# Pinning the order of three engines in the input norm, and splitting the load of the constants

## Chip, cores and metric

The kernel runs on one core of a Trainium2 chip. The metric is the device time of one execution in microseconds (us), the median of several runs. The engines are named as in the profile: PE is TensorE, PEld its weight loads, DVE is VectorE, ACT is ScalarE, POOL is GpSimd, SP is SyncE (here it only issues DMAs).

## What is computed

One layer of a bidirectional encoder on 512 tokens of width 1024, in float32. Cut to its frame, the reference is:

```python
x = x + token_mixer(rmsnorm(x, norm_mix), w_in, ...)
x = x + cross_attention(rmsnorm(x, norm_xattn), rmsnorm(mem, norm_mem), ...)
x = x + squared_relu_mlp(rmsnorm(x, norm_mlp), w_up, w_down)
return rmsnorm(x, norm_final)

def rmsnorm(x, g):
    y = x * lax.rsqrt(jnp.mean(x * x, axis=-1, keepdims=True) + 1e-6)
    return y * g
```

The change touches only the first line: the RMS norm of the input ahead of the token mixer, and the loads that go with it. The mixer begins with one large input projection, `proj = rmsnorm(x) @ w_in + b_in`; its columns are the values, queries, forget gates and so on of two groups of recurrent heads.

## The kernel before

**Number format.** Every large product is made of three products. Each operand is split into a high part (a copy rounded to the fast matmul format, made by ScalarE) and a low part (the rest, made by VectorE: source minus high part). `split_out` (L222) writes both; `mm3` (L226) multiplies high by high (L227), high by low (L228) and low by high (L229) into one PSUM bank. So every operand costs one pass of ScalarE and one of VectorE before TensorE can use it.

**Weights.** All weight matrices lie in DRAM as blocks of 128 x 1024 in the order of use (`SEQ`). `load` (L198) fetches a block through SyncE's queue into one of three buffers `st`; `split` (L205) makes its high and low parts (`wh`, `wl`, three buffers each). `weights` (L214) hands out a block and asks for the splits of the next two and the load of a third.

**The input norm (L288 to L304).** The tokens come in four tiles of 128 x 1024 (`xtile`, in the trace `as`), loaded by SyncE with the first two weight blocks between them (L134, L202). For each tile ScalarE squares it and sums the rows (L292, with a short instruction that reads the accumulator), VectorE turns the sum into a mean (L167), and GpSimd raises it to the power -0.5 (L169; `rstd_of`). VectorE then scales each half of the tile by that and by the gain row (L297). The gain row stands in two PSUM banks, `gmix`, into which TensorE multiplied it at the start (L143). TensorE transposes each half in four blocks of 128 x 128 into PSUM (L300), using the identity `ident`, and `split_out` makes the high and low halves of the transposed tile `xT` (L302). The first weight blocks are split after tiles 0 and 1 (L304).

**The first projection (L317, `proj_t`, L253).** It takes four weight blocks, each covering two of the eight 128-row blocks of the width, and all four token tiles: 4 x 4 x 2 x 3 = 96 products of 128 x 128 by 128 x 512. The first three weight blocks go through all tiles one after the other; the last goes tile by tile. The gate projection follows (L462, with the operands the other way round in the trace: `mm<-xT,wh` instead of `mm<-wh,xT`).

**Small constants.** `cs` (128 x 392) holds the identity (columns 0 to 127), two masks and a selector; it is loaded in one DMA from ScalarE's queue (L138). `vc` (128 x 117) holds biases, gains and convolution weights, and `lm` is a mask kept as bytes, which is loaded as floats and converted. Both are handled in `small_setup` (L145), after the four tiles, by DMAs from SyncE's queue (L147, L148), a VectorE copy for the mask (L149), and some instructions on 8 columns (L152 to L159). The mask is used by the masked copy at L383, the biases after the gate projection (L468 onwards).

**What sets the order.** Except in the last part of the kernel (the MLP, where TensorE's order is the program's), the order of the instructions on each engine is chosen by a planner: it plays the program through with estimated times and takes what it believes to be ready first, earlier lines and lines under `tc.high_priority()` before others. On the chip each engine then keeps to its list, and waits at the head of it. Only L294 to L302 and the later weight splits have high priority in this stage.

Of the kernel before, what the change touches and what calls it, by code (L numbers as in the profile page):

```python
# [13 lines left out]
AF = mybir.ActivationFunctionType  # L14
ALU = mybir.AluOpType
# [3 lines left out]
P = 128  # L19
S = 512  # L20
D = 1024
# [18 lines left out]
C_ID, C_MF, C_MB, C_SEL, NC1 = 0, 128, 256, 384, 392  # L40
C_INC, C_SUF, C_ISUF, C_PRE, C_ONE = 0, 128, 256, 384, 512
NC_ = NC1 + 640
LEVELS = (1, 2, 4, 8, 16, 32, 64)
# [36 lines left out]
def trunk(ctx: ExitStack, tc: tile.TileContext, x, mem, wpk, vec, cst, lmask, rmask, rows, out):  # L80
    nc = tc.nc
# [4 lines left out]
    v, sc, gp, pe = nc.vector, nc.scalar, nc.gpsimd, nc.tensor  # L86
    cnt = [0]

    def nm(s):
        cnt[0] += 1  # L90
        return f"{s}_{cnt[0]}"

    def T(tag, w, bufs, dt=F32):
        return (sb if w == 516 else big).tile([P, w], dt, tag=tag, name=nm(tag), bufs=bufs)

    def mmb():
        return psm.tile([P, 512], F32, tag="mm", name=nm("mm"))

    def smb():
        return pss.tile([P, 512], F32, tag="sm", name=nm("sm"))  # L100

    def tiny(w):
        return sb.tile([P, w], F32, tag=f"tiny{w}", name=nm("tiny"), bufs=2 if w == 8 else 6)

    def ap(t, off, *dims):
        a = t[:, :]
        return bass.AP(a.tensor, a.offset + off, [list(a.ap[0])] + [list(d) for d in dims])
# [12 lines left out]
    cs = sb.tile([P, NC1], F32, name="cs")  # L120
    vc = sb.tile([P, NV], F32, name="vc")
    lm = sb.tile([P, len(LEVELS) * P], U8, name="lm")
    ident = cs[:, C_ID:C_ID + P]
    grow1 = RG()
    xin = [A16(), A16()]
    xtile = [xin[t // 2][:, (t % 2) * 1024:(t % 2) * 1024 + 1024] for t in range(4)]
# [8 lines left out]

    load_x(0)
    nc.scalar.dma_start(out=grow1[0:1, :], in_=rows[0:1, :])
    nc.scalar.dma_start(out=cs, in_=cst[:, 0:NC1])  # L138
    one1 = misc[0:1, 63:64]
    gp.memset(one1, 1.0)  # L140
    gmix = [mmb(), mmb()]
# [2 lines left out]

    def small_setup():  # L145
        lmf = A4()
        nc.sync.dma_start(out=vc, in_=vec)  # L147
        nc.sync.dma_start(out=lmf[:, 0:len(LEVELS) * P], in_=lmask)  # L148
        v.tensor_copy(lm, lmf[:, 0:len(LEVELS) * P])  # L149
        le, lr = tiny(8), tiny(8)  # L150
        lg = vc[:, V_LB:V_LB + 8]
        v.tensor_tensor(out=le, in0=lg, in1=lg, op=ALU.subtract)  # L152
        sc.activation(le, le, AF.Exp)
        v.reciprocal(lr, le)
        v.tensor_tensor(out=le, in0=le, in1=lr, op=ALU.mult)
        v.tensor_tensor(out=lb[:, 0:8], in0=le, in1=le, op=ALU.subtract)
        v.tensor_scalar(out=lb[:, 8:16], in0=lb[:, 0:8], scalar1=-1.0, scalar2=1.0, op0=ALU.mult, op1=ALU.add)
        v.tensor_copy(selr, cs[:, C_SEL:C_SEL + 8])
        v.tensor_scalar(out=negb, in0=vc[:, V_FF:V_FF + 8], scalar1=-1.0, scalar2=None, op0=ALU.mult)  # L159
# [5 lines left out]
    def rstd_of(ss, w, n):  # L165
        ms = tiny(w)
        v.tensor_scalar(out=ms, in0=ss, scalar1=1.0 / n, scalar2=EPS, op0=ALU.mult, op1=ALU.add)  # L167
        r = tiny(w)
        gp.tensor_tensor(out=r, in0=ms, in1=nh.to_broadcast([P, w]), op=ALU.pow)  # L169
        return r, ms  # L170
# [27 lines left out]
    def load(i):  # L198
        if i >= NSTREAM or i in st_tiles:
            return  # L200
        t = T("st", 1024, 3)
        nc.sync.dma_start(out=t, in_=wpk[i])  # L202
        st_tiles[i] = t

    def split(i):  # L205
        if i >= NSTREAM or i in hl_tiles:
            return
        load(i)
        s = st_tiles[i]
        hi, lo = T("wh", 1024, 3, F32R), T("wl", 1024, 3, F32R)  # L210
        split_out(hi, lo, s)
        hl_tiles[i] = (hi, lo)
# [9 lines left out]
    def split_out(dst_hi, dst_lo, src):  # L222
        sc.activation(dst_hi, src, AF.Copy)  # L223
        v.tensor_tensor(out=dst_lo, in0=src, in1=dst_hi.bitcast(F32), op=ALU.subtract)  # L224
# [7 lines left out]
    def xk(tiles, n=512):  # L232
        o = []
        for k in range(8):
            t = tiles[k // 4]
            b = (k % 4) * 2 * n
            o.append((t[:, b:b + n], t[:, b + n:b + 2 * n]))
        return o

    def proj_d(mat, c0, xs, n=512, count=2):  # L240

        for j in range(count):
            wh, wl = weights(("d", mat, 0, c0 + P * j))
            ps = mmb()
            for k in range(8):
                z = slice(k * P, k * P + P)
                mm3(ps[:, :n], wh[:, z], wl[:, z], xs[k][0], xs[k][1], k == 0, k == 7)
                if k == 3:
                    tick()
            yield ps  # L250
            tick()
# [29 lines left out]
    xT = XT()  # L281
# [4 lines left out]
    load_x(3)  # L286

    junk = G4()  # L288
    for t in range(4):
        xt = xtile[t]  # L290
        ss = tiny(1)
        sc.activation(junk, xt, AF.Square, accum_out=ss)  # L292
        r, _ = rstd_of(ss, 1, D)
        with tc.high_priority():  # L294
            for g in range(2):
                xg = xt[:, g * 512:g * 512 + 512]
                v.scalar_tensor_tensor(out=xg, in0=xg, scalar=r, in1=gmix[g], op0=ALU.mult, op1=ALU.mult)  # L297
                ps = smb()
                for k in range(4):
                    pe.transpose(ps[:, k * P:k * P + P], xg[:, k * P:k * P + P], ident)  # L300
                p3 = ps[:, :].rearrange("p (k t) -> p k t", t=P)
                split_out(ap(xT[g], t * P, [1024, 4], [1, P]), ap(xT[g], 512 + t * P, [1024, 4], [1, P]), p3)  # L302
        if t < 2:
            split(t)  # L304
    small_setup()
    xs = xk(xT)


# [397 lines left out]
    for t in range(2):  # L706
# [6 lines left out]
        ss = tiny(1)  # L713
        v.tensor_tensor(out=ss, in0=s2_[:, 0:1], in1=s2_[:, 1:2], op=ALU.add)
        r, _ = rstd_of(ss, 1, D)
# [6 lines left out]
    for k in range(8):  # L722
        ps = smb()
        for t in range(2):
            pe.transpose(ps[:, t * P:t * P + P], mt[t][:, k * P:k * P + P], ident)
        g = vc[:, V_MEM + k:V_MEM + k + 1]
# [217 lines left out]
    for f in range(4):  # L944
# [3 lines left out]
        for p in range(4):  # L948
            a = []
            for j in range(2):  # L950
                ps, = proj_d("up", 1024 * f + P * (p + 4 * j), x3, count=1)
# [65 lines left out]
        while n < len(JOBS):  # L1017
            p, g = JOBS[n]
# [104 lines left out]
```

## Time and profile before

| | |
|---|---|
| median of 3 runs | 877.57 us (877.56 to 878.74) |
| the profiled execution | 877.47 us |
| its span, first to last instruction | 875.7 us |
| TensorE busy | 853.6 us (97%) |
| VectorE busy | 576.2 us (66%) |
| ScalarE busy | 415.5 us (47%) |
| GpSimd busy | 67.4 us (8%) |

Busy time of TensorE counts pipelined products whose ends are modelled, so the pace of the products (start to start) tells more than their length: 0.39 us each in the rows, but one starts every 0.227 us. Times in the timeline are counted from the start of the span. In a row of the timeline the first number is the start, the second the length of the group that the row merges; `x2` is the number of instructions; what stands in brackets is the idle time of the engine before it and what ended that. `out<-in` names the tiles by the program's names.

### The profile page before, as it was taken

How to read it: one execution, taken by the hardware profiler on the slowest of the kernel's cores; microseconds unless marked ns; L12 is line 12 of the kernel's file. 1: busy time of each engine (PE TensorE's matmuls, PEld its weight loads, DVE VectorE, ACT ScalarE, POOL GpSimd, SP SyncE). 2: the span in 40 equal slices, each digit the busy share in tenths (PEclk: the TensorE clock that was granted, in tenths of full speed). 3: DMA queues.
4: the chain of work that ended last, by engine and by line, in shares of the span. 5: the costliest groups of instructions: out<-in, count | busy, mean ns of one | idle time of the engine just before them, and what ended most of it. 6: DMA issues, size and time to landing. Idle time of an engine off the chain costs nothing.

```text
span 875.7 us, 11191 instructions
## 1 busy us (share of the span) xinstructions
PE 853.6 (97%) x4198; PEld 709.3 (81%) x4198; DVE 576.2 (66%) x1006; ACT 415.5 (47%) x758; POOL 67.4 (8%) x114
## 2 busy tenths in 40 slices
PE   7999999999999999999999999999999999999995
PEld 5887888888887886888888887888888888888884
DVE  5557688779536987654655445776667656766675
ACT  5235343353358658534544355553355345435544
POOL 2000000010001000000000200002200310121001
PEclk9999999999999999999999999999999999999998
DMA  7322222311234223352212772238945993598322
GB/s 261 135 98 79 73 73 73 117 63 50 73 99 117 97 98 120 121 169 84 85 51 71 194 190 82 92 116 212 284 143 127 238 279 109 150 284 217 115 55 96
DMA packets 32680, 113.58 MB, mean 130 GB/s; under 512 B 3761, under 2 KB 3889, under 8 KB 32626
## 3 DMA queue, kind: packets, MB, share of 16 engines
q1 hardware_dynamic: 23120, 78.84, 26.1%
q0 software_dynamic: 9216, 33.56, 17.2%
q8 instruction: 33, 0.54, 0.2%
q10 hardware_dynamic: 290, 0.47, 0.1%
q14 instruction: 21, 0.17, 0.1%
HBM read 110.76 MB, written 2.10 MB: 129 GB/s over the span
## 4 chain that ended last, share of the span: by engine, by line
PE 49%; DVE 1%; ACT 0%; POOL 0%; issue 0%; POOLq 0%; ACTq 0%
PE mm L228 10%; PE mm L229 10%; PE mm L227 10%; PE sm L997 5%; PE sm L999 5%; PE sm L998 5%; PE mm L999 1%; PE mm L998 1%; PE mm L997 1%; PE sm L229 1%; PE sm L228 1%; PE sm L227 1%; PE sm L770 0%; PE sm L827 0%; DVE vv L922 0%; ACT t L756 0%
## 5 line engine op out<-in xcount | busy, mean ns | idle before, releaser
L223 ACT ACTIVATE wh<-st 128x1024 fp32r<-128x1024 f32 x133 | 140.9, 1059 | 233.1 <-PE mm L228 115.4
L224 DVE TENSOR_TENSOR wl<-st,wh 128x1024 fp32r<-128x1024 f32 x133 | 162.7, 1223 | 124.3 <-ACT wh L223 120.6
L227 PE MATMUL mm<-xT,wh 128*128 128x512 f32 x552 | 219.7, 399 | 0.0
L228 PE MATMUL mm<-xT,wh 128*128 128x512 f32 x552 | 216.4, 392 | 0.2 <-DVE xT L776 0.2
L229 PE MATMUL mm<-xT,wl 128*128 128x512 f32 x552 | 215.8, 391 | 0.0
L228 PEld LDWEIGHTS mm<-xT,wh 128*128 128x128 f32 x552 | 103.8, 188 | 22.7 <-DVE xT L776 2.0
L229 PEld LDWEIGHTS mm<-xT,wl 128*128 128x128 f32 x552 | 103.6, 188 | 21.7 <-issue 0.2
L227 PEld LDWEIGHTS mm<-xT,wh 128*128 128x128 f32 x552 | 103.8, 188 | 21.4 <-issue 1.2
L891 POOL DMA_DIRECT2D as<-in_wpk x48 | 36.6, 772 | 312.1 <-DVE wl L224 188.1
L955 DVE SCALAR_TENSOR_TENSOR t<-mm,rg 128x512 f32<-128x512 f32 x32 | 22.1, 691 | 55.2 <-PE mm L229 55.0
L229 PE MATMUL mm<-wh,yT 128*128 128x512 f32 x128 | 50.6, 395 | 0.0
L227 PE MATMUL mm<-wh,yT 128*128 128x512 f32 x128 | 50.5, 394 | 0.0
L228 PE MATMUL mm<-wl,yT 128*128 128x512 f32 x128 | 50.0, 391 | 0.0
L999 PE MATMUL sm<-wh,yT 128*128 128x512 f32 x128 | 49.8, 389 | 0.0
L998 PE MATMUL sm<-wl,yT 128*128 128x512 f32 x128 | 49.8, 389 | 0.0
L997 PE MATMUL sm<-wh,yT 128*128 128x512 f32 x128 | 49.8, 389 | 0.0
L223 ACT ACTIVATE wh<-as 128x1024 fp32r<-128x1024 f32 x24 | 25.5, 1062 | 33.3 <-PE sm L999 23.7
L224 DVE TENSOR_TENSOR wl<-as,wh 128x1024 fp32r<-128x1024 f32 x24 | 29.4, 1225 | 13.9 <-ACT wh L223 13.9
L378 PEld LDWEIGHTS sm<-a,t 128*128 128x128 f32 x224 | 30.1, 191 | 2.2 <-ACT t L368 0.4
L930 DVE TENSOR_TENSOR vv<-vv,sm 128x512 f32<-128x512 f32 x48 | 31.0, 680 | 1.2 <-PE sm L999 1.2
L368 ACT ACTIVATE t<-a 128x512 f32<-128x512 f32 x28 | 18.4, 674 | 26.3 <-DVE a L431 23.8
L378 PE MATMUL sm<-a,t 128*128 128x128 f32 x224 | 30.9, 285 | 0.0
(258 smaller groups left out, 1513.5 us busy)
## 6 DMA issues: line engine op xcount, KB each, us to landing
st<-in_wpk SPq DMA_DIRECT2D x133, 512.0 KB, 3.3
as<-in_wpk POOLq DMA_DIRECT2D x48, 512.0 KB, 6.7
gate<-in_wpk POOLq DMA_DIRECT2D x16, 512.0 KB, 7.2
as<-in_x SPq DMA_DIRECT2D x4, 512.0 KB, 6.5
vv<-in_x SPq DMA_DIRECT2D x8, 256.0 KB, 4.3
out<-vv SPq DMA_DIRECT2D x7, 256.0 KB, 2.3
a<-in_mem SPq DMA_DIRECT2D x2, 512.0 KB, 3.9
t<-in_rows SPq DMA_DIRECT2D x2, 256.0 KB, 5.9
```

Source lines behind the costliest of these rows:

```text
L223: sc.activation(dst_hi, src, AF.Copy)
L224: v.tensor_tensor(out=dst_lo, in0=src, in1=dst_hi.bitcast(F32), op=ALU.subtract)
L227: pe.matmul(ps, lhsT=ah, rhs=bh, start=first, stop=False)
L228: pe.matmul(ps, lhsT=ah, rhs=bl, start=False, stop=False)
L229: pe.matmul(ps, lhsT=al, rhs=bh, start=False, stop=last)
L378: pe.matmul(ps[:, z], lhsT=kc[:, z], rhs=ap(q2, w * P, [2 * L, P // (2 * L)], [512 + L, 2], [1, L]), start=True, stop=True)
L891: gp.dma_start(out=dst, in_=wpk[idx], **kw)
L930: v.tensor_tensor(out=z, in0=z, in1=ps, op=ALU.add if sign > 0 else ALU.subtract)
L955: v.scalar_tensor_tensor(out=y, in0=ps, scalar=0.0, in1=rrow[:, 0:512], op0=ALU.max, op1=ALU.mult)
L997: pe.matmul(ps, lhsT=ah, rhs=bh, start=new, stop=False, **fl)
L998: pe.matmul(ps, lhsT=ah, rhs=bl, start=False, stop=False, **fl)
L999: pe.matmul(ps, lhsT=al, rhs=bh, start=False, stop=end and k == 1, **fl)
```

## The change

Three things. First, for ScalarE, VectorE and GpSimd the input norm is put into the order of the program, so that these engines run it as written, ahead of everything else; TensorE and the DMA queues are still planned. The steps are cut into three functions: `x_stat` (Square, mean, power), `x_scale` (two scalings, eight transposes), `x_split` (high and low halves), and written out in a chosen sequence together with the splits of the first three weight blocks and `small_setup`. Second, the identity is loaded by a DMA of its own, followed on ScalarE's queue by `vc` (which was on SyncE's queue) and by the rest of `cs`. Third, the copy that turns the mask into bytes moves from VectorE to GpSimd. No arithmetic changes.

```diff
@@ -135,7 +135,9 @@
 
     load_x(0)
     nc.scalar.dma_start(out=grow1[0:1, :], in_=rows[0:1, :])
-    nc.scalar.dma_start(out=cs, in_=cst[:, 0:NC1])
+    nc.scalar.dma_start(out=ident, in_=cst[:, C_ID:C_ID + P])
+    nc.scalar.dma_start(out=vc, in_=vec)
+    nc.scalar.dma_start(out=cs[:, P:NC1], in_=cst[:, P:NC1])
     one1 = misc[0:1, 63:64]
     gp.memset(one1, 1.0)
     gmix = [mmb(), mmb()]
@@ -144,9 +146,8 @@
 
     def small_setup():
         lmf = A4()
-        nc.sync.dma_start(out=vc, in_=vec)
         nc.sync.dma_start(out=lmf[:, 0:len(LEVELS) * P], in_=lmask)
-        v.tensor_copy(lm, lmf[:, 0:len(LEVELS) * P])
+        gp.tensor_copy(lm, lmf[:, 0:len(LEVELS) * P])
         le, lr = tiny(8), tiny(8)
         lg = vc[:, V_LB:V_LB + 8]
         v.tensor_tensor(out=le, in0=lg, in1=lg, op=ALU.subtract)
@@ -286,23 +287,44 @@
     load_x(3)
 
     junk = G4()
-    for t in range(4):
-        xt = xtile[t]
+    rs_x, px = {}, {}
+
+    def x_stat(t):
         ss = tiny(1)
-        sc.activation(junk, xt, AF.Square, accum_out=ss)
-        r, _ = rstd_of(ss, 1, D)
-        with tc.high_priority():
-            for g in range(2):
-                xg = xt[:, g * 512:g * 512 + 512]
-                v.scalar_tensor_tensor(out=xg, in0=xg, scalar=r, in1=gmix[g], op0=ALU.mult, op1=ALU.mult)
-                ps = smb()
-                for k in range(4):
-                    pe.transpose(ps[:, k * P:k * P + P], xg[:, k * P:k * P + P], ident)
-                p3 = ps[:, :].rearrange("p (k t) -> p k t", t=P)
-                split_out(ap(xT[g], t * P, [1024, 4], [1, P]), ap(xT[g], 512 + t * P, [1024, 4], [1, P]), p3)
-        if t < 2:
-            split(t)
-    small_setup()
+        sc.activation(junk, xtile[t], AF.Square, accum_out=ss)
+        rs_x[t], _ = rstd_of(ss, 1, D)
+
+    def x_scale(t):
+        for g in range(2):
+            xg = xtile[t][:, g * 512:g * 512 + 512]
+            v.scalar_tensor_tensor(out=xg, in0=xg, scalar=rs_x[t], in1=gmix[g], op0=ALU.mult, op1=ALU.mult)
+            px[t, g] = smb()
+            for k in range(4):
+                pe.transpose(px[t, g][:, k * P:k * P + P], xg[:, k * P:k * P + P], ident)
+
+    def x_split(t):
+        for g in range(2):
+            p3 = px[t, g][:, :].rearrange("p (k t) -> p k t", t=P)
+            split_out(ap(xT[g], t * P, [1024, 4], [1, P]), ap(xT[g], 512 + t * P, [1024, 4], [1, P]), p3)
+
+    with tc.high_priority(), tc.manual_schedule(engines={mybir.EngineType.DVE, mybir.EngineType.Activation, mybir.EngineType.Pool}):
+        x_stat(0)
+        x_scale(0)
+        split(0)
+        x_stat(1)
+        x_split(0)
+        x_scale(1)
+        x_stat(2)
+        x_split(1)
+        x_scale(2)
+        split(1)
+        x_split(2)
+        x_stat(3)
+        x_scale(3)
+        x_split(3)
+        load(2)
+        split(2)
+        small_setup()
     xs = xk(xT)
 
 
```

## Rows read from the trace of the kernel before

**Rows 1.** The page, part 1: busy time and share of each engine.

```profile
PE 853.6 (97%) x4198; PEld 709.3 (81%) x4198; DVE 576.2 (66%) x1006; ACT 415.5 (47%) x758; POOL 67.4 (8%) x114
```

**Rows 2.** Windows (start:end, length, busy per engine, PEclk, DMA share, GB/s).

```profile
9.40:13.80 4.40, 4.40 (x16) 3.77 (x17) 3.33 (x6) 2.61 (x5) 0.55 (x1) 1.00 0.96 323
...
18.00:24.20 6.20, 5.79 (x34) 4.58 (x33) 5.41 (x13) 2.49 (x5) 2.07 (x8) 1.00 0.14 53
...
24.20:37.60 13.40, 13.40 (x60) 11.08 (x59) 7.02 (x11) 3.19 (x3) 0.00 (x0) 1.00 0.46 156
```

**Rows 3.** Timeline (start, length), all engines, up to the first weight product.

```profile
4.67 1.06 ACT L292 ACTIVATE gate<-as 128x1024 f32<-128x1024 f32 x1 [1.87 <-DMA as<-in_x]
...
6.08 0.56 POOL L169 TENSOR_TENSOR tiny<-tiny,misc 128x1 f32<-128x1 f32 x1 [5.11 <-DVE tiny L167]
...
6.38 1.06 ACT L223 ACTIVATE wh<-st 128x1024 fp32r<-128x1024 f32 x1 [0.56 <-DMA st<-in_wpk]
...
7.46 1.22 DVE L224 TENSOR_TENSOR wl<-st,wh 128x1024 fp32r<-128x1024 f32 x1 [0.67 <-ACT wh L223]
...
7.78 1.06 ACT L292 ACTIVATE gate<-as 128x1024 f32<-128x1024 f32 x1 [0.35 <-DMA as<-in_x]
...
8.61 1.40 DVE L297 SCALAR_TENSOR_TENSOR as<-as,tiny,mm 128x512 f32<-128x512 f32 x2
...
9.40 1.97 PE L300 MATMUL sm<-cs,as 128*128 128x128 f32 x8 [3.39 <-DVE as L297]
...
11.20 0.79 PE L227 MATMUL mm<-wh,xT 128*128 128x512 f32 x1
```

**Rows 4.** Timeline, TensorE, to the end of the first projection.

```profile
12.22 1.05 PE L300 MATMUL sm<-cs,as 128*128 128x128 f32 x4
...
14.32 0.60 PE L300 MATMUL sm<-cs,as 128*128 128x128 f32 x4
...
14.67 0.48 PE L227 MATMUL mm<-wh,xT 128*128 128x512 f32 x1
...
20.79 0.63 PE L300 MATMUL sm<-cs,as 128*128 128x128 f32 x4 [0.41 <-issue]
...
37.60 0.39 PE L227 MATMUL mm<-xT,wh 128*128 128x512 f32 x1
```

**Rows 5.** Timeline, VectorE and GpSimd, tiles 1 to 3.

```profile
12.00 0.74 DVE L297 SCALAR_TENSOR_TENSOR as<-as,tiny,mm 128x512 f32<-128x512 f32 x1
...
14.88 1.23 DVE L224 TENSOR_TENSOR wl<-st,wh 128x1024 fp32r<-128x1024 f32 x1 [0.25 <-ACT wh L223]
...
16.69 0.62 DVE L149 CAST lm<-a 128x896 uint8<-128x896 f32 x1
...
16.92 0.79 POOL L169 TENSOR_TENSOR tiny<-tiny,misc 128x1 f32<-128x1 f32 x1 [6.22 <-DVE tiny L167]
...
17.75 1.40 DVE L297 SCALAR_TENSOR_TENSOR as<-as,tiny,mm 128x512 f32<-128x512 f32 x2 [0.44 <-POOL tiny L169]
...
24.16 1.18 DVE L224 TENSOR_TENSOR wl<-st,wh 128x1024 fp32r<-128x1024 f32 x1
```

**Rows 6.** Groups by line, 4 to 26 us (busy us, mean ns, idle before).

```profile
L224 DVE TENSOR_TENSOR xT<-sm,xT 128x512 fp32r<-128x512 f32 x8 | 5.4, 687 | 0.8 <-ACT xT L223 0.5
...
L223 ACT ACTIVATE xT<-sm 128x512 fp32r<-128x512 f32 x8 | 4.8, 596 | 5.7 <-PE sm L300 5.6
...
L292 ACT ACTIVATION_READ_ACCUMULATOR gate<-as 128x1 f32 x4 | 0.8, 189 | 0.0
```

**Rows 7.** DMA issues, 0 to 40 us (count, KB, us to landing).

```profile
cs<-in_cst ACTq DMA_DIRECT2D x1, 196.0 KB, 5.2
...
vc<-in_vec SPq DMA_DIRECT2D x1, 58.5 KB
```

**Rows 8.** Timeline near 98 us; waits of TensorE, 40 to 100 us.

```profile
98.07 0.73 DVE L383 COPY_PREDICATED as<-lm,sm 128x512 f32<-128x512 uint8 x1
...
PE sm L556 <- DVE a L545: 1.7, 1, 1.7
```

## The prediction

> **What bounds the kernel now.** I read the engines first, then windows, then the timeline of the opening. TensorE is busy 97% of the span [rows 1], so only time that TensorE loses can be won. From 24.2 to 37.6 us it runs with no gap: 13.40 us for 60 products, of which one had begun before, so 59 pitches of 0.227 us [rows 2]. The page gives the profiled execution 877.47 us round a span of 875.7; the median of three runs is 877.57, 0.10 above it.
>
> The change touches the first projection alone. That projection has 96 products (four weight pairs, four token tiles, two blocks, three products). The first starts at 11.20 [rows 3], and the next projection, its operands the other way round, starts at 37.60 [rows 4]: 26.40 us. The 96 products are 21.79 us. Six groups of four transposes (tiles 1 to 3) lie between them. A group costs 14.67 − 14.32 = 0.35 us, and I estimate 0.44 with the weights that must be loaded again after it; six are 2.64. So 26.40 − 24.43 = 1.97 us are lost. Of that, the stretch 11.20 to 14.32 holds six products and one group, 1.80 us of work in 3.12: 1.32 lost [rows 3, 4]. Another 0.41 is the wait ahead of the transposes at 20.79 [rows 4]; 0.24 is small change. Everything before 11.20 is lost too, where earlier work could stand.
>
> **The change part by part.**
>
> *VectorE's order for tile 0.* The inverse root of tile 0 is ready at 6.08 + 0.56 = 6.64, yet VectorE does the low half of weight block 0 first (7.46, 1.22 us) and scales at 8.61 [rows 3]. In the new order the two scalings run at about 6.7 to 8.1, the low half at 8.1 to 9.3. The eight transposes, 9.40 to 11.20 before [rows 3], run from 7.45 to 9.25.
>
> *The Square of tile 1 ahead of tile 0's split.* This is a new wait: ScalarE is in order, and tile 0's high halves now stand behind a Square that waits for the landing of x1, at 7.78 [rows 3]. It ends at 7.78 + 1.06 + 0.19 = about 8.95 [rows 3, 6]; without it the high half could start near 8.6, so it costs 0.3 us. High halves of 0.60 each then run 8.95 to 10.15 [rows 6], and the first product starts at 9.6 rather than 11.20: **1.6 us earlier**.
>
> *Tiles 1 to 3 and weight pairs 1, 2.* Now each tile's scaling stands behind both low halves of the tile before it. Low halves of 0.69 and scalings of 0.70 (1.40 for two) [rows 3, 6] give on VectorE: tile 0's low halves to 10.95, scaling 1 to 12.35, transposes and high halves of tile 1 from 11.7 to 13.8, low halves to 14.6, scaling 2 14.6 to 16.0 (17.75 to 19.15 before [rows 5]), weight low half 1 16.0 to 17.2 (before, 14.88 to 16.11 [rows 5]: **1.1 us later**), low halves 2 to 18.6. Tile 3's Square, behind tile 2's high halves on ScalarE, is done by 18.4, its root by 19.35, scaling 3 19.4 to 20.8, its low halves to 22.75, weight low half 2 23.1 to 24.3 (before, 24.16 to 25.34 [rows 5]: 1.0 earlier).
>
> *What TensorE makes of it.* From 9.6, 24.43 us of work and the opening loss of 1.32 give 35.35. The late weight half 1 adds a dry spot. Until 17.2 there are 12 products of tiles 0 and 1 (2.72), four groups (1.76), the opening loss and about four products of tile 2 (0.9): 6.7 us of work in 7.6, so 0.9 dry. For waits inside the order I keep 0.4, as at 20.79 before [rows 4]. The projection ends at 36.65, **0.95 us earlier** than 37.60. After weight half 2 there remain at least 47 products, so the end can't lie before 24.3 + 10.7 = 35.0; that floor is the best case.
>
> *Clock of the opening.* The eight transposes at 9.40 take 0.225 us each, against 0.35 / 4 = 0.09 at 14.32 [rows 3, 4], and the first products are as slow, though the granted clock reads 1.00, which is 2.4 GHz, there too [rows 2]. So the row's clock doesn't tell the opening; the pace does. I carry the 1.32 over as it is. The Trainium skill, "TensorE: Matmul & The Clock Gate", Part 1, says that "the default state is throttled, and activity releases the throttle". The rows agree as to the order (slow after idling, then fast), and by that rule the slow part would start with the transposes at 7.45 and end about as much earlier, for a projection end near the floor; that is the first rival below.
>
> *DMAs.* The constant block, with the identity in it, landed 5.2 us after its issue [rows 7]; the identity alone lands no later. The first transposes wait for VectorE's scaling and not for it [rows 3], and at 7.45 they still would if it came by then; so this alone wins nothing. The vector of small constants goes from SyncE, behind the fourth tile, to ScalarE's queue. Two more issues there cost ScalarE nothing: it is idle until 4.67, waiting for x0 [rows 3]. But 58.5 KB move ahead of later tiles [rows 7]; at the 323 GB/s of a window whose DMA share is 0.96 [rows 2], that is up to 0.2 us on x1, which now stands on the path. At the other end it is a gain of up to 0.4: the tail of the constant block, 132 of its 196 KB, now goes behind both. I take 0, between these ends. SyncE's queue only loses an issue. The Trainium skill, "DMA: Bandwidth & Descriptors", Issuing engines are not separate DMA queues, says that DMAs of all issuing engines share the same 16 engines and interleave; by it the sum would be 0.2 us worse.
>
> *Mask copy to GpSimd, small set-up last.* VectorE loses a 0.62 us copy at 16.69, during which the power on GpSimd took 0.79 instead of 0.56 [rows 3, 5]; both were off the new chain. How long GpSimd takes for the copy no row shows; from nothing to 10 us, the first use of the mask at 98.07 covers it [rows 8]. I take 0. If the small set-up ran late, the biases wanted after the next projection would be next; over 10 us cover it.
>
> *After 37.6.* The work there is the same, but a planner orders it, and it plans anew from another start. Its largest single wait is 1.7 us near the gate chain [rows 8]. I bound this at 1 us either way and take 0.
>
> Sum: 877.47 − 0.95 = 876.5, and with the 0.10 to the median **876.6 us**. About 0.2% (1.76 us) is what a measurement of this kernel can tell from no change, so this is the middle case.
>
> **The rivals.**
>
> *1. The clock comes up with the earlier start (faster).* The opening loss shrinks from 1.32 to about 0.3 and nothing is lost in the order: 9.6 + 24.43 + 0.3 + 0.9 = 35.25, just above the floor. That is 2.35 earlier: 875.2. For it: the slow stretch began with TensorE's first steady work at 9.40. Against: the new TensorE work is sparse until 17.2, and the floor hangs on a chain of some 20 steps with no slack.
>
> *2. The dry spot eats the start (no change, up to a little slower).* If the slow pace lasts through the sparse part, six more products (1.36) and three groups at twice 0.44 (1.32) cost 2.7 more, of which 0.9 fill the dry spot: 36.65 + 1.8 = 38.4, or 878.4; where it lasts through half of that, 37.5 and 877.5. For it: a sparse TensorE came just before the slow stretch in the old profile. Against: that TensorE stood still for 3.39 us [rows 3]; no gap I foresee is longer than 1.
>
> *3. TensorE's own order holds transposes back (slower).* Only three engines are pinned; TensorE's order stays the planner's. Before, the second scaling of tile 1 ended at 12.74, and its transposes ran at 14.32, 1.6 us later, behind products [rows 4, 5]. Now VectorE's next scaling and weight half 2 hang on those transposes. If tile 2's second group, ready at 16.0, is placed behind the 12 products of weight pair 1, which need the half ready at 17.2, it runs at 19.9, and the chain slips by up to 4.5: end 35.0 + 4.5 = 39.5, or 879.5. It decides once the chain slips over 2.6 us (37.6 − 35.0). Against: at 20.79 the planner had put nothing in front of a group that wasn't ready, and TensorE waited [rows 4].
>
> *4. The order was already nearly this one.* For tiles 2 and 3 the pinned order differs little; then only the 1.6 us of the start count, and the dry spot against them; this lies inside the forecast.
>
> **How the numbers follow.** Forecast, with its neighbours down to nothing: 0.50, own range 875.9 to 877.5. Rival 2: 0.12. Rival 1: 0.27. Rival 3: 0.11. So faster 0.27, same 0.62, slower 0.11. The range reaches to rival 1 with 0.2 for the planner below it, 875.0, and above over rival 2 with part of the new plan, 878.7; rival 3 is left out.
>
> **What would show it.** Right: first scaling near 6.7, first product near 9.6, weight low half 1 near 17.2 and weight low half 2 near 24.3, start of the next projection at 36.2 to 37. Clock: the pitch reaches 0.227 before 13 (rival 1) or after 15 (rival 2). Rival 3 shows as a transpose group that starts over 1.5 us after its scaling. Wrong altogether: the next projection starts by the forecast, and the end of the span doesn't follow it; then the plan behind 37.6 has changed, and TensorE's waits there tell where.

## The result, and the profile after

The changed kernel takes 879.24 us (median of 22 runs) against 877.75 us of the kernel before (22 runs): a ratio of 1.0015, 95% interval 1.0009 to 1.0021. It is 1.5 us slower: the interval lies above 1, but the step is less than the 1.76 us that the prediction took for the least that can be told from no change. One of the 22 runs of the changed kernel took 3531 us and does not count in the ratio. The forecast was 0.95 us faster, with a range up to 878.7; the time lies above it.

The page of the changed kernel, part 1, answers to [rows 1]. TensorE has the same work and a longer span round it:

```profile
span 877.6 us, 11194 instructions
...
PE 856.0 (98%) x4198; PEld 709.4 (81%) x4198; DVE 576.0 (66%) x1005; ACT 415.6 (47%) x758; POOL 68.1 (8%) x115
```

The profiled execution took 879.38 us round a span of 877.6, 1.9 us more than before. The next projection starts at 39.45 instead of 37.60 [rows 4], 1.85 later. So nothing to speak of changed behind it: the loss lies in the opening. This is the timeline of the changed kernel from the first scaling to the next projection (start, length, engine, line; line numbers are those of the new kernel: L300 is the scaling, L303 the transposes, L224 and L225 high and low halves, L228 to L230 the products):

```profile
6.60 1.41 DVE L300 SCALAR_TENSOR_TENSOR as<-as,tiny,mm 128x512 f32<-128x512 f32 x2 [0.67 <-POOL tiny L170]
...
7.40 1.97 PE L303 MATMUL sm<-cs,as 128*128 128x128 f32 x8 [1.43 <-DVE as L300]
...
9.20 0.80 PE L228 MATMUL mm<-wh,xT 128*128 128x512 f32 x1
...
11.07 0.63 PE L229 MATMUL mm<-wl,xT 128*128 128x512 f32 x1
11.50 0.63 PE L230 MATMUL mm<-wh,xT 128*128 128x512 f32 x1
11.93 1.59 PE L303 MATMUL sm<-cs,as 128*128 128x128 f32 x8
...
14.97 0.40 PE L229 MATMUL mm<-wl,xT 128*128 128x512 f32 x1
15.21 0.39 PE L230 MATMUL mm<-wh,xT 128*128 128x512 f32 x1
...
16.17 1.22 DVE L225 TENSOR_TENSOR wl<-st,wh 128x1024 fp32r<-128x1024 f32 x1
...
19.61 1.41 DVE L300 SCALAR_TENSOR_TENSOR as<-as,tiny,mm 128x512 f32<-128x512 f32 x2 [0.73 <-POOL tiny L170]
...
20.51 0.47 PE L228 MATMUL mm<-wh,xT 128*128 128x512 f32 x1 [0.46 <-DVE as L300]
...
21.98 0.27 PE L303 MATMUL sm<-cs,as 128*128 128x128 f32 x1
22.00 0.48 PE L228 MATMUL mm<-wh,xT 128*128 128x512 f32 x1
22.32 0.27 PE L303 MATMUL sm<-cs,as 128*128 128x128 f32 x1
...
23.31 0.60 ACT L224 ACTIVATE xT<-sm 128x512 fp32r<-128x512 f32 x1 [4.61 <-PE sm L303]
...
26.17 0.27 PE L303 MATMUL sm<-cs,as 128*128 128x128 f32 x1
...
26.48 0.60 ACT L224 ACTIVATE xT<-sm 128x512 fp32r<-128x512 f32 x1 [2.57 <-PE sm L303]
26.97 2.94 ACT L224 ACTIVATE wh<-st 128x1024 fp32r<-128x1024 f32 x3
...
28.06 3.50 DVE L225 TENSOR_TENSOR wl<-st,wh 128x1024 fp32r<-128x1024 f32 x3 [0.26 <-ACT wh L224]
...
28.08 1.19 PE L228 MATMUL mm<-wh,xT 128*128 128x512 f32 x4 [0.70 <-ACT wh L224]
...
39.45 0.39 PE L228 MATMUL mm<-xT,wh 128*128 128x512 f32 x1
```

Down to 19.61 it is the chain of the forecast: first scaling at 6.60 (forecast 6.7), first product at 9.20 (9.6; before, 11.20 [rows 3]), weight low half 1 from 16.17 (16.0), scaling 3 from 19.61 (19.4). Then it breaks. Tile 3 is scaled by 21.02, but its transposes run one or two at a time between products, from 21.98 to 26.4. ScalarE stands idle 4.61 and 2.57 us ahead of the two high halves. Behind them, in the order now fixed, stands the high half of weight pair 2, at 26.97; and TensorE, which by then has nothing else, waits 0.70 for it.

Windows of the changed kernel, cut at those points (columns as in [rows 2]):

```profile
9.20:13.67 4.47, 4.32 (x15) 3.37 (x14) 2.76 (x7) 2.28 (x5) 1.10 (x2) 1.00 0.96 305
13.67:17.45 3.78, 3.36 (x17) 2.28 (x17) 3.78 (x6) 2.34 (x4) 0.00 (x0) 1.00 0.63 258
17.45:21.98 4.53, 4.07 (x17) 2.98 (x17) 2.70 (x5) 1.25 (x3) 2.95 (x9) 1.00 0.33 116
21.98:28.08 6.10, 5.40 (x28) 3.89 (x26) 1.41 (x3) 2.20 (x4) 0.00 (x0) 1.00 0.01 3
28.08:39.45 11.37, 11.30 (x49) 9.04 (x49) 7.52 (x14) 3.11 (x4) 0.00 (x0) 1.00 0.53 184
```

TensorE starts 6, 8, 16, 18 and 48 products in them, and two groups of transposes in the first, the second and the fourth. At 0.227 and 0.44 us, the forecast's prices, that is 24.43 us of work in 30.25. Lost are 2.23, 1.08, 0.90, 1.13 and 0.47, together 5.8 against 1.97 before. The start came 2.0 earlier, the loss grew by 3.85, and the difference is the 1.85.

The clock column of the windows prints 1.00 also where the trace has no record of the clock. The first record in the trace, of 1.00, stands at 13.05 us here and at 13.76 in the kernel before; ahead of it products start 0.43 us apart, and from 14.97 on 0.24. So the first window is slow for TensorE's pace, whatever its column says.

### The profile page after: what moved, and what is told of

Same layout as the page of the kernel before. It is cut to its first block, busy times and chain, and to the rows that moved or that the text cites. A ratio compares the mean times of both kernels' runs of the same rounds, so it can differ in the third digit from the quotient of the medians.

```text
span 877.6 us, 11194 instructions
## 1 busy us (share of the span) xinstructions
PE 856.0 (98%) x4198; PEld 709.4 (81%) x4198; DVE 576.0 (66%) x1005; ACT 415.6 (47%) x758; POOL 68.1 (8%) x115
## 4 chain that ended last, share of the span: by engine, by line
PE 85%; issue 6%; DVE 4%; ACT 2%; POOL 1%; DMA 1%; POOLq 0%; ACTq 0%; DVEq 0%
PE mm L229 18%; PE mm L228 18%; PE mm L230 18%; PE sm L1019 5%; PE sm L1021 5%; PE sm L1020 5%; PE sm L400 3%; PE sm L653 2%; PE sm L638 2%; PE sm L433 1%; POOL tiny L170 1%; DVE wl L225 1%; PE mm L1019 1%; PE mm L1021 1%; PE mm L1020 1%
## 5 line engine op out<-in xcount | busy, mean ns | idle before, releaser
L224 ACT ACTIVATE wh<-st 128x1024 fp32r<-128x1024 f32 x133 | 140.7, 1059 | 227.9 <-PE mm L229 117.3
L225 DVE TENSOR_TENSOR wl<-st,wh 128x1024 fp32r<-128x1024 f32 x133 | 162.6, 1224 | 120.4 <-ACT wh L224 116.9
L228 PE MATMUL mm<-xT,wh 128*128 128x512 f32 x552 | 219.6, 398 | 0.0
L230 PE MATMUL mm<-xT,wl 128*128 128x512 f32 x552 | 215.8, 391 | 0.0
L230 PEld LDWEIGHTS mm<-xT,wl 128*128 128x128 f32 x552 | 103.6, 188 | 21.8 <-issue 0.2
L228 PEld LDWEIGHTS mm<-xT,wh 128*128 128x128 f32 x552 | 103.8, 188 | 21.4 <-issue 1.2
L230 PE MATMUL mm<-wh,yT 128*128 128x512 f32 x128 | 50.6, 395 | 0.0
L228 PE MATMUL mm<-wh,yT 128*128 128x512 f32 x128 | 50.5, 394 | 0.0
L224 ACT ACTIVATE wh<-as 128x1024 fp32r<-128x1024 f32 x24 | 25.5, 1062 | 33.6 <-PE sm L1021 24.0
L225 DVE TENSOR_TENSOR wl<-as,wh 128x1024 fp32r<-128x1024 f32 x24 | 29.4, 1226 | 14.1 <-ACT wh L224 14.1
L390 ACT ACTIVATE t<-a 128x512 f32<-128x512 f32 x28 | 18.4, 673 | 26.4 <-DVE a L453 25.5
```

The lines of the kernel that those rows point to most:

```text
L228: pe.matmul(ps, lhsT=ah, rhs=bh, start=first, stop=False)
L230: pe.matmul(ps, lhsT=al, rhs=bh, start=False, stop=last)
```

## The experiments

The questions were, which part of the change does it, and whether TensorE's scattered transposes (theory A), the place of weight pair 2 in ScalarE's and VectorE's order (B) or the moved loads (C) make the loss. "Next projection" is the start of its first product in the profile. The kernel before ran beside each group of experiments, with medians of 877.40, 877.43 and 877.61 us. The ratios weigh all runs of both kernels; they are not the quotient of the two medians, which jumps where the times stand on two levels.

**1. Loads and mask copy alone**, the old loop kept:

```diff
-    nc.scalar.dma_start(out=cs, in_=cst[:, 0:NC1])
+    nc.scalar.dma_start(out=ident, in_=cst[:, C_ID:C_ID + P])
+    nc.scalar.dma_start(out=vc, in_=vec)
+    nc.scalar.dma_start(out=cs[:, P:NC1], in_=cst[:, P:NC1])
...
-        nc.sync.dma_start(out=vc, in_=vec)
-        v.tensor_copy(lm, lmf[:, 0:len(LEVELS) * P])
+        gp.tensor_copy(lm, lmf[:, 0:len(LEVELS) * P])
```

> Only the loads and the mask copy of the change, the loop of before kept. Theory A (the transposes of tile 3, scattered among products by TensorE's planner, are what costs the changed kernel its 1.5 us): the loads cost nothing by themselves, 877 to 878.3 us, with the planner's new order as the only reason for a difference. Rival C (the moved loads cost it): 879 us, and the Square of tile 1 later than 7.8 us.

Measured: 882.96 us, ratio 1.0062 (1.0048 to 1.0076); next projection at 41.27. The profiled run took 881.20 us, 3.7 more than that of the kernel before, as the next projection starts 3.67 later; the four other runs took 882.9 to 883.5 (for the levels, see below). Both theories missed. The timeline of this kernel shows the load of `vc`, the Square of tile 1 and VectorE:

```profile
1.75 0.44 ACTq L139 DMA_DIRECT2D vc<-in_vec  x1
...
7.55 1.06 ACT L293 ACTIVATE gate<-as 128x1024 f32<-128x1024 f32 x1 [0.57 <-DMA as<-in_x]
...
8.46 0.17 DVE L153 TENSOR_TENSOR tiny<-vc 128x8 f32<-128x8 f32 x1 [2.65 <-DMA vc<-in_vec]
...
10.08 0.17 DVE L159 CAST selr<-cs 128x8 fp32r<-128x8 f32 x1 [1.36 <-DMA cs<-in_cst]
...
10.16 1.23 DVE L225 TENSOR_TENSOR wl<-st,wh 128x1024 fp32r<-128x1024 f32 x1
...
11.31 1.40 DVE L298 SCALAR_TENSOR_TENSOR as<-as,tiny,mm 128x512 f32<-128x512 f32 x2
```

The planner, left free, put the small set-up at the head of VectorE's list, and there it waits for `vc`, which landed 6.7 us after its issue, and then for the rest of `cs`. The first scaling starts at 11.31 instead of 8.61 [rows 3]. The token tiles were not late, for the Square of tile 1 started at 7.55, earlier than before; late were the constants, for an instruction that stood ahead of the work. In the changed kernel the fixed order puts the small set-up last (its first instruction on VectorE runs at 31.47) and hides this: there the loads need the order.

**2. The order alone**, loads and mask copy as before (the same diff, reversed).

> Only the fixed order of the three engines, loads and mask copy as before. Theory A: as slow as the changed kernel or nearly, 878.3 to 879.3 us; here the planner scatters only the first four of the eight transposes of tile 3, so the high halves of tile 3 should be done about 1 to 2 us earlier than 27.1 us and the start of the next projection lie between 37.6 and 39.5. Rival C: back at 877.7.

Measured: 880.11 us, ratio 1.0016 (1.0006 to 1.0026); next projection at 39.24, as expected by A. The high halves of tile 3 were done at 25.85, 1.2 earlier. The order alone is slower without the moved loads, so C can't be the whole cause. The median is above what A gives; the runs stand on two levels, five at 877.5 to 878.3 and six at 880.1 to 880.8, of which more below.

**3. Tile 3's transposes kept together**: the products that stood among them are queued behind the last one (`last_t`) on TensorE.

```diff
-                part(t, q, w)
+                with (tc.issue_after(last_t[0].ins) if mat == "in" and c0 == 1536 and (t == 3 or (t == 2 and q > 0) or q > 1) else ExitStack()):
+                    part(t, q, w)
...
-                pe.transpose(px[t, g][:, k * P:k * P + P], xg[:, k * P:k * P + P], ident)
+                last_t[0] = pe.transpose(px[t, g][:, k * P:k * P + P], xg[:, k * P:k * P + P], ident)
```

> The changed kernel, with the products that stood between the eight transposes of tile 3 queued behind them on TensorE. Theory A: high halves of tile 3 done at about 24 rather than 27.1 us, low half of weight pair 2 at about 26.2 rather than 29.3, the next projection at about 37.8 rather than 39.45: 877.6 us, no different from the kernel before. Rival B (the late weight pair 2 is late for the order of ScalarE and VectorE, whatever TensorE does): at most the 0.9 us that scattered transposes cost in pitch comes back, 878.4 us.

Measured: 879.19 us, ratio 1.0008 (0.9999 to 1.0017); next projection at 37.90, 1.55 earlier than with the change, as theory A said. The timeline of this kernel:

```profile
21.75 1.03 PE L304 MATMUL sm<-cs,as 128*128 128x128 f32 x8
...
22.38 1.09 ACT L224 ACTIVATE xT<-sm 128x512 fp32r<-128x512 f32 x2 [3.90 <-PE sm L304]
...
24.45 1.22 DVE L225 TENSOR_TENSOR wl<-st,wh 128x1024 fp32r<-128x1024 f32 x1 [0.15 <-ACT wh L224]
```

High halves done at 23.5, weight low half 2 at 25.7. But the median didn't follow. Its runs stand on two levels, five at 877.1 to 877.5 and six at 879.2 to 880.1, and the profile is one of the upper ones.

**4. Weight pair 2 split earlier**, ahead of tile 3's Square and scaling; transposes left to the planner.

```diff
         x_split(2)
+        load(2)
+        split(2)
         x_stat(3)
         x_scale(3)
         x_split(3)
-        load(2)
-        split(2)
```

> The changed kernel, with the split of weight pair 2 moved ahead of tile 3's Square and scaling. Theory A: little, since transposes of tile 3 stay scattered and now their scaling comes 1.2 us later: 878.8 to 879.8 us. Rival B: products of pair 2 for tiles 0 and 1 fill TensorE while tile 3 is on its way, no wait near 27 to 28 us, and the next projection starts before 38.5: 878.2 us or less.

Measured: 878.74 us, ratio 1.0005 (0.9995 to 1.0014); next projection at 37.68, with no wait near 27 to 28 us: rival B, by the profile; the median is above B's 878.2. Again there are two levels, three runs at 876.6 and eight at 878.5 to 879.7. The edit did one thing more: the planner now strings out only three of tile 3's transposes and puts five in a row, done by 25.3 instead of 26.4. The timeline of this kernel:

```profile
23.53 0.27 PE L303 MATMUL sm<-cs,as 128*128 128x128 f32 x1
...
24.56 0.71 PE L303 MATMUL sm<-cs,as 128*128 128x128 f32 x5
```

So it shortens the scattering as well as the way of pair 2.

**5. Both edits**, but with the products of pair 2 for tiles 0 and 1 no longer queued behind the transposes (`or q > 1` left out), so that they can stand in there.

> The changed kernel with both edits: weight pair 2 split ahead of tile 3's Square, and the transposes of tile 3 kept together. Theory A and B together (scattered transposes and a late pair 2 each make TensorE wait, and either one filled hides the other): hardly better than either alone, next projection at 37.2 to 37.7 and the undisturbed times at 876.2 to 876.7. Rival (the two losses add): next projection at 36.4 or earlier, undisturbed times at 875.5.

Measured: 879.07 us, ratio 1.0011 (1.0003 to 1.0020); next projection at 37.64; two runs at 876.6 to 876.8 and nine at 878.6 to 879.5. Together they are no better than experiment 4 alone (876.6 on the lower level) and better than experiment 3 (877.1 to 877.5): once pair 2 is early, the scattering that was left costs nothing that these runs show.

**What the two levels are.** The windows behind the gate chain tell. The kernel before (columns as in [rows 2]):

```profile
67.00:70.50 3.50, 1.82 (x10) 1.20 (x10) 3.49 (x4) 2.21 (x3) 0.00 (x0) 1.00 0.00 0
70.50:74.00 3.50, 3.50 (x17) 2.88 (x16) 3.46 (x7) 2.11 (x3) 0.00 (x0) 1.00 0.16 28
```

And experiment 3 in the same windows:

```profile
67.00:70.50 3.50, 1.83 (x11) 1.25 (x10) 3.49 (x4) 2.21 (x3) 0.00 (x0) 1.00 0.00 0
70.50:74.00 3.50, 3.50 (x10) 2.69 (x10) 3.46 (x6) 2.11 (x3) 0.00 (x0) 0.51 0.10 18
```

In both, TensorE is busy for half of the first window: it waits 1.7 us there [rows 8]. In the second, it stands at a granted clock of 1.00 in one and of 0.51, the 1.2 GHz level, in the other, and does 10 products instead of 17. Seven products are 1.6 us. The kernel before has the two levels as well, 877.1 to 877.8 and 878.5 to 879.0 (one run 879.9). The mean granted clock of each run parts them: of the 80 runs of the kernel before beside the experiments, the 28 of the upper level all have 0.994, the 52 of the lower 0.995 to 0.997. A comparison of medians thus also counts how many runs of each kernel fell to which level. Of the changed kernel's runs only four have 0.994. Without them its median is 879.17; that of the 13 runs of the kernel before, of the 22 above, that are on the lower level is 877.34, 1.8 less, which agrees with the 1.85 of the two profiles. So the levels don't make the loss.

**6. The kernel before, without that wait**: four transposes of the gate chain two steps later in the program.

```diff
         ml["ar"] = ar
+        yield
+        yield
         ps = smb()
```

> The kernel before, with the four transposes of the gate chain's stabiliser placed two steps later in the program, so that TensorE no longer waits for the VectorE scans near 67.5 us. Theory D (in part of the executions the TensorE clock falls to 1.2 GHz for a while after that wait, near 70 to 77 us, and this makes the two levels of times, 877.3 and 878.7): no row of reduced clock there, one level of times, at 877.3 - 1.7 = 875.6 or lower. Rival (the two levels come from the opening): the wait of 1.7 us is saved in every run, and two levels 1.4 us apart remain, at 875.6 and 877.0.

Measured: 875.44 us (875.05 to 875.73, one level), ratio to the kernel before 0.9975 (0.9966 to 0.9984). The same windows of this kernel:

```profile
67.00:70.50 3.50, 3.50 (x18) 2.88 (x17) 3.45 (x4) 2.21 (x3) 0.00 (x0) 1.00 0.00 0
70.50:74.00 3.50, 3.50 (x18) 2.67 (x17) 3.50 (x6) 2.09 (x3) 0.00 (x0) 1.00 0.21 51
```

No wait, full clock, one level: theory D.

**7. The changed kernel with the same edit.**

> The changed kernel with the same edit of the gate chain. Theory D: one level of times. The change's own cost then shows without the clock: with theory A it is the 1.85 us by which the next projection starts later, so 1.5 to 2.0 us above the run of the kernel before with the same edit. Rival (the change's median is slower only because more of its executions meet the reduced clock): within 0.5 us of it.

Measured: 877.39 us (876.51 to 877.81), ratio to the kernel before 0.9992 (0.9983 to 1.0001). Against experiment 6 that is 1.95 us more, with no run of the one within the other's spread: the change's own cost, free of the clock near 70 us. The two profiles of this pair give 1.40: next projection at 38.79 against 37.39, in runs of 876.96 and 875.57 us. The runs here are not on one level: five lie at 876.5 to 877.0, the profiled one among them, and six at 877.4 to 877.8. Where that comes from is told below.

**8. Both edits, and the gain row copied out of its PSUM banks**; the products of tile 2 with pair 1 no longer have to wait for the transposes either. The accumulators of the projection and the two banks of the gain row come from the same four; tiles 2 and 3 get theirs only when the gain row has been read for the last time, by the scaling of tile 3. The row at 20.51 above shows that wait, 0.46 us for L300.

```diff
         x_stat(2)
+        for g in range(2):
+            sc.activation(gsb[:, g * 512:g * 512 + 512], gmix[g], AF.Copy)
+            gsrc[g] = gsb[:, g * 512:g * 512 + 512]
         x_split(1)
```

> As with both edits, and the gain row is copied from its two PSUM banks to SBUF by ScalarE in its idle time before tile 1's high halves, so tiles 2 and 3 are scaled from SBUF and the two banks are free for products of tiles 2 and 3 after the scaling of tile 1. Theory E (TensorE has nothing to do near 17 to 20.5 us because the accumulators of tiles 2 and 3 lie in the banks that hold the gain row until tile 3 is scaled): no wait of 0.5 us for the scaling near 20 us, the next projection 0.4 to 0.8 us earlier than with both edits alone. Rival (those products come later anyway, and the copies delay tile 1): no earlier.

Measured: 878.15 us, ratio 1.0002 (0.9994 to 1.0011); next projection at 37.40, 0.24 earlier than in experiment 5. The wait for the scaling near 20 us had shrunk to 0.2 us in experiment 5 already, where pair 2 stands in. What goes here is the wait for weight low half 1. Experiment 5 has

```profile
17.33 0.50 PE L229 MATMUL mm<-wl,xT 128*128 128x512 f32 x1 [0.41 <-DVE wl L225]
```

and experiment 8

```profile
17.24 0.19 PEld L228 LDWEIGHTS mm<-wh,xT 128*128 128x128 f32 x1 [0.28 <-ACT xT L224]
17.24 0.50 PE L228 MATMUL mm<-wh,xT 128*128 128x512 f32 x1
```

The product at 17.24 is one of tile 2, and starts as soon as that tile's first high half is there. So the banks did hold tile 2 back. It brought less than expected. Part of that may be the clock of the opening: its first record stands at 13.60 here and at 12.77 in experiment 5. The lower runs are at 876.5 to 877.2, in experiment 5 at 876.6 and 876.8: no gain that these runs can tell.

**Four more with the gate edit**, where the times have no second level from 70 us. Tile 3's transposes together:

> The changed kernel with tile 3's transposes kept together, and the gate chain's transposes two steps later, so that the reduced clock near 70 us doesn't blur the comparison. Against 877.39 us of the changed kernel and 875.44 of the kernel before, both with the gate edit. Theory A (scattered transposes cost the 1.95 us): 875.4 to 876.0, most of it back. Rival B (the late pair 2 costs it in any case): 876.6 or more.

Weight pair 2 early:

> The changed kernel with weight pair 2 split ahead of tile 3's Square and scaling, transposes left scattered where the planner put them, and the gate edit. Theory B': scattering costs only because nothing else is ready (pair 2's split stands behind tile 3's high halves); with pair 2 ready TensorE is not idle and the time is 875.0 to 875.6, no worse than with the transposes kept together. Theory A alone: 876.6 or more.

The order alone:

> Only the fixed order of the three engines with the gate edit; loads and mask copy as before. If the order makes the whole loss: 876.5 to 877.5; the planner scatters only the first four transposes here. If the moved loads and mask copy carry a part of it: nearer to 875.4.

All edits:

> Pair 2 early, tile 3's transposes kept together, gain row copied out of the accumulator banks, gate edit. If the waits of the opening add up as in the profile of the run without the gate edit (next projection at 37.40 against 38.79 of the changed kernel with the gate edit): 875.44 us of the kernel before with the gate edit, minus 0 to 0.8 us, so 874.6 to 875.4; it would be the fastest of all.

| with the gate edit | median (us) | runs | against experiment 6 |
|---|---|---|---|
| kernel before (6) | 875.44 | 875.05 to 875.73 | |
| changed kernel (7) | 877.39 | 876.51 to 877.81 | +1.95 |
| order alone | 876.31 | 875.96 to 877.97 | +0.87 |
| changed, transposes together | 876.14 | 875.50 to 876.54 | +0.70 |
| changed, pair 2 early | 875.31 | 874.99 to 876.49 | -0.13 |
| changed, all edits | 874.91 | 874.84 to 875.31 | -0.53 |

Keeping the transposes together gives back 1.25 of the 1.95 us; splitting pair 2 earlier gives back all of it, with the first three transposes of tile 3 still scattered. The lower levels of experiments 3 and 4, 877.4 and 876.6, differ as these two do. So theory A alone is too strong: in the changed kernel scattering hurts because the only other work, pair 2, is queued behind tile 3. How much each of the two would cost by itself isn't shown, since the early pair 2 also shortened the scattering, and the grouped transposes also brought pair 2 forward (low half ready at 25.7 instead of 29.3). With the transposes together 0.70 us remains, a little above what was expected; the wait for the banks (0.5 us) is still there.

The order alone is 0.87 us slower by its median, 0.2 less than expected. But its runs, too, stand in two groups, six at 876.0 to 876.3 and five at 877.0 to 878.0, and its profile, one of the upper, has the next projection at 38.90, as late as the whole change. Whether the moved loads carry a part of the 1.95 us these runs don't tell. With all edits it is the fastest kernel of the study, ratio to the kernel before 0.9963 (0.9951 to 0.9976), nearly all of which is the gate edit.

**The spread that is left.** Up to the next projection, each kernel of the table has the same order of TensorE's instructions as its twin without the gate edit. The profiles of such a pair are thus two executions of one opening. In the table, the first number is the time of the first clock record (1.00), the second the next projection:

| opening of | without the gate edit | with it |
|---|---|---|
| kernel before | 13.76, 37.60 | 14.39, 37.39 |
| changed kernel | 13.05, 39.45 | 11.67, 38.79 |
| order alone | 14.87, 39.24 | 13.89, 38.90 |
| changed, transposes together | 12.53, 37.90 | 13.22, 38.30 |
| changed, pair 2 early | 12.89, 37.68 | 10.68, 36.80 |
| changed, all edits | 13.60, 37.40 | 11.27, 36.65 |

In all five pinned openings the execution whose clock came up earlier is ahead at the next projection, by 0.3 to 0.9 us. Tile 1's eight transposes show it in the changed kernel: 1.59 us at 11.93 above, and in experiment 7

```profile
11.74 1.04 PE L303 MATMUL sm<-cs,as 128*128 128x128 f32 x8
```

And with the gate edit the difference of two profiled runs is that of their next projections to about 0.1 us. So a difference between two single profiles of these openings is sure only to such an amount, and the measures of what the change costs run from 1.40 to 1.95 us.

## Why the prediction was wrong

- *VectorE's order for tile 0, and the new wait for x1.* Right: first product 2.0 us earlier (forecast 1.6). Tile 1's Square started at 7.38, not 7.78.
- *DMAs.* Right at nothing, but the case that I bounded did not arise. In the changed kernel `vc` was issued behind the start of tile 0's Square, not ahead of the later tiles:

```profile
4.60 0.35 ACTq L139 DMA_DIRECT2D vc<-in_vec  x1
```

  Experiment 1 is the case: `vc` issued at 1.75, and tile 1's Square at 7.55, no later than before.
- *The chain of tiles 1 and 2 and weight pair 1.* Right to 0.3 us, and there was a dry spot as forecast: 1.08 lost up to 17.45 (forecast 0.9), of which the profile puts 0.42 to the late weight half 1 itself.
- *Clock of the opening.* I carried over a loss of 1.32; in the profile it was 2.23 up to 13.67. The first products start 0.43 us apart (11.07 to 11.50), tile 1's transposes take 0.20 each (11.93), and later products start 0.24 apart (14.97 to 15.21). In the kernel before, that pace was reached at 13.85:

```profile
13.85 0.40 PE L228 MATMUL mm<-wl,xT 128*128 128x512 f32 x1
...
14.09 0.40 PE L229 MATMUL mm<-wh,xT 128*128 128x512 f32 x1
```

  The start came 2.0 us earlier and the clock's first record only 0.7 (13.05 against 13.76), so the slow stretch grew. This took 0.9 of the sum. The Trainium skill, "TensorE: Matmul & The Clock Gate", Part 1, says that activity releases the throttle; the rows bear out the order of slow and fast and no more. Rival 1's sign, full pace before 13, just fails in this profile and shows in that of experiment 7, with the same order of TensorE. So how much of rival 1 an execution gets is a matter of luck, for which I had no term.
- *What TensorE makes of it.* **The step that failed.** I took tile 3's transposes to run when tile 3 is scaled, and weight half 2 to be ready at 24.3. It was ready at 29.3, as TensorE's own list, which the change doesn't pin, had the eight transposes strung out among fourteen products. The losses after 21.98 (1.13 and 0.47) weren't in the sum. That is rival 3's mechanism, which I gave 0.11 and priced at +1.9 on the next projection; it came at +1.85, though at tile 3 and not tile 2. That the two agree so well is partly luck: the chain slipped by 5.0 us, not 4.5, and after weight half 2 there remained 44 products, not the 47 of the floor, as four of pair 2 ran at 28.08, ahead of it.
- *The accumulators.* A second thing left out in the same step: I let tile 2's products fill TensorE before 17.2, but their bank wasn't free until the first scaling of tile 3 was done, 19.61 + 0.74 = 20.35. Before, the high half of weight pair 2 was made at 16.49, and two early products of it stood in there; the new order moved just that split to the end. The kernel before:

```profile
16.49 1.05 ACT L223 ACTIVATE wh<-st 128x1024 fp32r<-128x1024 f32 x1
...
19.68 0.70 PE L227 MATMUL mm<-wh,xT 128*128 128x512 f32 x2
```

  I saw pair 2 only as a bound on the end (a floor of 35.0), not as the one thing that TensorE could do meanwhile. Experiment 4, where six products fill the stretch from 19.7 to 21.1, shows it.
- *The mask copy.* Right at nothing: 0.93 us on GpSimd, off the path.
- *After 37.6.* Right in the profile; the median also held what I hadn't seen, the two levels.
- *Slips in the working.* Rival 1's sum is 35.23, not 35.25, and ScalarE isn't idle until 4.67: it waits for x0 the last 1.87 us before that [rows 3]. Neither moved the forecast.

Point by point in the sum, each loss less what the forecast had for it: a forecast end of 36.65, plus 0.9 (opening), 0.2 (dry spot), 0.5 (bank) and 1.6 (tile 3 and pair 2), less 0.4 (earlier start), gives 39.45.

## What to carry to other kernels

When some engines get a fixed order and one stays planned, read the planned one's list as well: an in-order engine that depends on it pays for each step that it puts late. Before moving a piece of work to the end, ask which engine would have used it as filler, and whether the other filler is free, down to the PSUM banks. Where runs stand on two levels, find the cause and take it out of both kernels before comparing them by a microsecond; and ask of a difference between two profiles whether two executions of one of the kernels differ as much.

## What the hardware showed that I had not expected

A single wait of 1.7 us in a TensorE stream that is otherwise full (1.82 of 3.50 us busy) was followed in some executions by a stretch at a granted clock of about a half, 10 products in 3.5 us instead of 17, and not in others of the same kernel. With the wait taken away, the kernel before ran on one level, 875.05 to 875.73, 2.0 us below its old median of 877.4, though the wait itself was 1.7. What decides in which executions the clock falls is open.

The opening has the like: the clock came up at times from 10.7 to 13.1 us in executions whose TensorE started its first transposes at 7.2 to 7.4 and ran the same list up to there (the changed kernel, experiments 4 and 7, and pair 2 early with the gate edit), and up to 0.9 us of that is still there at the next projection. That fits the spread of 1.3 us in experiment 7; no run here isolates it.
